# Moving register loads behind a run's output matmuls, and dropping a copy at the end of a sort, in a gather-scatter kernel

## The chip, the cores and the metric

The kernel runs on one core of one Trainium2 chip. The metric is the device time of the whole program in microseconds (us). Before the change it was 990.08 us (median of 3 runs, 989.51 to 990.09).

Two clocks appear. The views of the profile count from the start of the span. Raw records of the trace carry an offset of 10.5 us: where the prediction says "load 673.60 to 674.87", the views have 663.05 to 664.32. Its "565 to 570 us" is also on the raw clock.

## The reference

There are 4096 nodes with 256 features and 262144 edges. Each edge adds its source's transformed features to its destination.

```python
N, E, D = 4096, 262144, 256
self_out = nodes @ w_self
msg = nodes[edges_src] @ w_msg
agg = np.zeros((N, D)); np.add.at(agg, edges_dst, msg)
return self_out + agg
```

## The kernel before

The kernel sorts the edges by keys of destination segment (512 nodes), source block (128 nodes), destination and source, all on VectorE with some transposes on PE. The sorted edges lie in 2048 columns of 128. One "run" is one pair of destination segment and source block: 8 segments x 32 blocks = 256 runs, about 8 columns each. For each column VectorE makes two one-hot tiles, and PE multiplies them into a count matrix in PSUM (the `ring`). Where in the ring a column lands depends on the data, so the address comes from a register, loaded from SBUF. Each run also has one head matmul at a fixed address, which opens its place in the ring, so a run has nine ring matmuls. When a run is complete, ScalarE copies its 128x512 counts to SBUF (`at`), and four output matmuls multiply them with the transformed features `Y`.

```python
LAG = 10
...
    def count_mm(ap, e, d, ci, start, after=()):          # one column into the ring
        mm = nc.tensor.matmul(out=ap, lhsT=e[...], rhs=d[...], start=start, stop=True, ...)
    def evac(r):                                          # ring -> at, on ScalarE
        ins = nc.scalar.copy(out=at[:], in_=ring[:, b:b + SEGW]).ins
    def apply_run(r):                                     # the output matmuls of run r
        s, b = divmod(r, T)
        if b == 0:  ...                                   # 8 more matmuls open a segment (self term)
        for t in range(SEGW // P):                        # 4 of them
            nc.tensor.matmul(
                out=out_ps[:, t, :], lhsT=at[:, t * P:(t + 1) * P], rhs=Y[:, b, :],
                start=False, stop=(b == T - 1), skip_group_check=True,
            )
        if b == T - 1:                                    # a segment ends
            o_sb = ohp.tile([P, SEGW // P, D], FP32, name="o_sb", tag="o_sb", bufs=2)
            for t in range(0, SEGW // P, 2):
                nc.scalar.copy(out=o_sb[:, t:t + 2, :], in_=out_ps[:, t:t + 2, :])
                nc.sync.dma_start(out_v[s, :, t:t + 2, :], o_sb[:, t:t + 2, :])
...
        for c in range(NCOL):
            ...                                           # one-hots for 16 columns; head matmul of a run
            if c % 8 == 0:
                regs = [nc.tensor.alloc_register(f"po{c}_{i}") for i in range(8)]
                nc.tensor.load(regs, poffs[0:1, c:c + 8])
            off = nc.tensor.snap(regs[c % 8], donate=True, min_val=0, max_val=RING * SEGW - W)
            count_mm(ring[:, bass.ds(off, W)], e, d, ci, False)
            while nev < NRUN and (8 * nev + 7 + MARG <= c or c == NCOL - 1):
                evac(nev)
                todo.append((c + LAG, nev))
                nev += 1
            while todo and (todo[0][0] <= c or c == NCOL - 1):
                apply_run(todo.pop(0)[1])
```

A run's evacuation is issued at column 1 of a later group of eight. With a lag of 10 its output matmuls follow column 3 of a group. With 14 they follow column 7, so the next instruction is the load for the next eight columns.

Of the kernel before, what the change touches and what calls it, by code (L numbers as in the profile page):

```python
# [21 lines left out]
SL = 16  # L22
RING = 6
MARG = 10
LAG = 10
NRUN = 256
SENT = float((1 << 24) - 1)

# [7 lines left out]
def _view3(ap: bass.AP, inner: int):  # L36
    return ap.rearrange("p (a b) -> p a b", b=inner)
# [3 lines left out]
def kernel(  # L41
# [9 lines left out]
    nc = tc.nc  # L51
# [4 lines left out]
    NCOL = E // P  # L56
# [3 lines left out]
    NSTAGE = 18  # L60
    JBITS = 11
    G16 = NCOL // P
# [14 lines left out]
    ident = const.tile([P, P], FP32, name="ident")  # L77
# [8 lines left out]
    XA = [sortp.tile([P, NCOL], FP32, name=f"XA{i}") for i in range(2)]  # L86
    XB = [sortp.tile([P, NCOL], FP32, name=f"XB{i}") for i in range(2)]

    HC = NCOL // 2
    for h in range(2):  # L90
# [17 lines left out]
            out=key, in0=dlo, scalar=128.0, in1=slo, op0=ALU.mult, op1=ALU.add  # L108
        )
        nc.vector.scalar_tensor_tensor(  # L110
            out=key, in0=dhi, scalar=float((1 << 21) - (1 << 16)), in1=key,
# [3 lines left out]
            out=key, in0=shi, scalar=float((1 << 16) - P), in1=key,  # L115
# [24 lines left out]
        out=hbase[:], in0=hbase[:], scalar1=float(SEGW), scalar2=None, op0=ALU.mult  # L140
# [6 lines left out]
        out=thr[:], in0=thr[:], scalar1=float(SEGW), scalar2=-0.5, op0=ALU.mult, op1=ALU.add  # L147
# [31 lines left out]
    for t in range(T):  # L179
        y_ps = psum_y.tile([P, D], FP32, name="y_ps", tag="y_ps", bufs=2)  # L180
        for k in range(2):
            nc.tensor.matmul(  # L182
                out=y_ps[:], lhsT=XT[:, k, t * P:(t + 1) * P], rhs=wcat[:, 2 + k, :],
# [2 lines left out]
        nc.scalar.copy(out=Y[:, t, :], in_=y_ps[:])  # L186

    psum_sort = tc.alloc_tile_pool(name="psum_sort", bufs=1, space=bass.MemoryType.PSUM)
    _run_sort(nc, psum_sort, XA, XB, ident, NCOL, NSTAGE, JBITS, G16)
    srt = XA[0]  # L190
    lane = XB[0]


    k16 = meta.tile([P, G16], FP32, name="k16")
# [26 lines left out]
        out=ex[:], in0=dl[:], scalar1=float(W - SEGW), scalar2=0.0, op0=ALU.add, op1=ALU.max  # L221
# [9 lines left out]
        out=wr[:], in0=sl[:], scalar1=float(RING), scalar2=float(-RING * SEGW),  # L231
# [3 lines left out]
        out=wr[:], in0=sl[:], scalar=float(SEGW), in1=wr[:], op0=ALU.mult, op1=ALU.add  # L235
# [20 lines left out]
    for h in range(2):  # L256
        nc.scalar.activation(
            out=junk[:], in_=gball[:], func=ACTF.Sign, bias=thr[:, h:h + 1], scale=-1.0,
# [3 lines left out]
        out=cnt[:], in0=cnt[:], scalar1=0.5, scalar2=float(NCOL // 2 - 1), op0=ALU.mult, op1=ALU.add  # L262
    )
    nc.vector.tensor_scalar(
        out=cidx[:], in0=cnt[:], scalar1=0.0, scalar2=None, op0=ALU.max
# [5 lines left out]
    for h in range(2):  # L271
        xh = meta.tile([P, P], FP32, name=f"xh{h}")
        nc.gpsimd.indirect_dma_start(
            out=xh[:], out_offset=None, in_=xs_dram[:, :],
# [61 lines left out]
    def evac(r):  # L336
        at = ohp.tile([P, SEGW], BF16, name="at", tag="at", bufs=4)
        b = (r % RING) * SEGW
        ins = nc.scalar.copy(out=at[:], in_=ring[:, b:b + SEGW]).ins  # L339
        tc.declare_no_dep(  # L340
            ins, group="count", keep=[last_mm[0]], reason="disjoint banks by static schedule"
        )
        tc.add_manual_dep(ins, last_mm[0].name, DEP, reason="run complete")
        tc.add_to_no_dep_group("evac", ins)
        evac_of[r] = ins
        at_of[r] = at
# [28 lines left out]
    with tc.manual_schedule():  # L375
# [5 lines left out]
        for c in range(NCOL):  # L381
# [19 lines left out]
# [4 lines that stand above are left out]
# [18 lines left out]
        out=hh[:], in0=rho[:], scalar1=float(SEGW), scalar2=float(SEGW), op0=ALU.mult, op1=ALU.add  # L423
    )
    nc.vector.scalar_tensor_tensor(
        out=v[:], in0=gn[:], scalar=1.0, in1=hh[:], op0=ALU.add, op1=ALU.min
# [3 lines left out]
        out=bad[:], in0=v[:], scalar=float(W), in1=bad[:], op0=ALU.is_gt, op1=ALU.add  # L430
# [3 lines left out]
        out=bad[:], in0=v[:], scalar=float(W - 1), in1=bad[:], op0=ALU.is_gt, op1=ALU.add  # L434
# [4 lines left out]
        out=bad[0:1, 0:1], in0=gi[0:1, 0:1], scalar=float(W - 1), in1=bad[0:1, 0:1],  # L439
# [71 lines left out]
def _run_sort(nc, psum, XA, XB, ident, NCOL, NSTAGE, JBITS, G16):  # L511

    cur = {"A": 0, "B": 0}

    def buf(lay):
        return XA[cur[lay]][:, 0:NCOL] if lay == "A" else XB[cur[lay]][:, 0:NCOL]

    def other(lay):
        return XA[1 - cur[lay]][:, 0:NCOL] if lay == "A" else XB[1 - cur[lay]][:, 0:NCOL]

    def flip_live(lay):
        cur[lay] = 1 - cur[lay]

    def evac(out_ap, in_ap, g):
        if g % 2 == 0:
            nc.scalar.copy(out=out_ap, in_=in_ap)  # L526
        else:
            nc.vector.tensor_copy(out=out_ap, in_=in_ap)

    def switch_A_to_B():  # L530
        src = buf("A")
        dst3 = buf("B").rearrange("q (p g) -> q p g", g=G16)
        for g in range(G16):
            tp = psum.tile([P, P], FP32, name="tp_sw", tag="tp", bufs=4)
            nc.tensor.transpose(tp[:], src[:, g * P:(g + 1) * P], ident[:])  # L535
            evac(dst3[:, :, g], tp[:], g)

    def switch_B_to_A():
        src3 = buf("B").rearrange("q (p g) -> q p g", g=G16)
        dst = buf("A")  # L540
        for g in range(G16):
            tp = psum.tile([P, P], FP32, name="tp_sw2", tag="tp", bufs=4)
            nc.tensor.transpose(tp[:], src3[:, :, g], ident[:])
            evac(dst[:, g * P:(g + 1) * P], tp[:], g)

    def flip(lay, blo, bhi):
        x = buf(lay)
        if lay == "A":
            assert blo <= JBITS - 1 and (bhi is None or bhi <= JBITS - 1)
            base_lo = blo  # L550
        else:
            assert blo >= 7
            base_lo = blo - 7
            if bhi is not None:
                assert bhi == blo + 1
        if bhi is None:
            per = 1 << (base_lo + 1)
            reg = _view3(x, per)[:, :, (1 << base_lo):per]
        else:
            per = 1 << (base_lo + 2)  # L560
            reg = _view3(x, per)[:, :, (1 << base_lo):(3 << base_lo)]
        nc.vector.tensor_scalar(out=reg, in0=reg, scalar1=-1.0, scalar2=None, op0=ALU.mult)

    def cpass(lay, fb):
        src = buf(lay)
        dst = other(lay)
        per = 1 << (fb + 1)
        s3 = _view3(src, per)
        d3 = _view3(dst, per)
        lo_s = s3[:, :, 0:(1 << fb)]  # L570
        hi_s = s3[:, :, (1 << fb):per]
        lo_d = d3[:, :, 0:(1 << fb)]
        hi_d = d3[:, :, (1 << fb):per]
        nc.vector.tensor_tensor(out=lo_d, in0=lo_s, in1=hi_s, op=ALU.min)  # L574
        nc.vector.tensor_tensor(out=hi_d, in0=lo_s, in1=hi_s, op=ALU.max)  # L575
        flip_live(lay)

    for s in range(1, NSTAGE + 1):
        if s <= JBITS - 1:
            if s == 1:  # L580
                flip("A", 1, None)
            else:
                flip("A", s - 1, s)
            for b in range(s - 1, -1, -1):
                cpass("A", b)
        else:
            switch_A_to_B()
            if s == NSTAGE:
                flip("B", NSTAGE - 1, None)
            else:  # L590
                flip("B", s - 1, s)
            for b in range(s - 1, 6, -1):
                cpass("B", b - 7)
            switch_B_to_A()
            for b in range(6, -1, -1):
                cpass("A", b)

    if cur["A"] != 0:
        nc.vector.tensor_copy(out=XA[0][:, 0:NCOL], in_=XA[cur["A"]][:, 0:NCOL])
        cur["A"] = 0  # L600
    switch_A_to_B()
    if cur["B"] != 0:
        nc.vector.tensor_copy(out=XB[0][:, 0:NCOL], in_=XB[cur["B"]][:, 0:NCOL])
        cur["B"] = 0


# [28 lines left out]
```

## Time and profile before

| stage | span (us) | what limits it |
|---|---|---|
| sort | 0 to 517 | VectorE, 92 to 98% busy by stretch from 40 us on |
| sorted keys to first count matmul | 517 to 548 | a chain of small work and DMAs |
| count loop, 256 runs | 548 to 979 | see below |
| tail | 979 to 988 | last copies, output, flag |

First, the table by stretch of the loop: start and end, length, then busy us (and instructions) of PE, PE weight load, VectorE, ScalarE, GpSimd, then the granted clock, the DMA share and GB/s.

```profile
700.00:800.00 100.00, 74.67 (x792) 60.46 (x790) 70.01 (x68) 36.92 (x64) 0.00 (x0) 1.00 0.04 12
```

Nothing is full in these 100 us. The clock is at full speed and DMA is nearly idle. The timeline of PE shows what a run looks like (start, us, engine, line, operation, count, and in brackets the idle time before it).

```profile
701.87 0.38 PE L323 MATMUL ring<-d_oh,e_oh 128*128 128x96 bf16 x5
702.66 0.57 PE L323 MATMUL ring<-d_oh,e_oh 128*128 128x96 bf16 x4 [0.41 <-issue]
703.07 0.60 PE L365 MATMUL out_ps<-Y,at 128*128 128x256 bf16 x4
703.50 0.38 PE L323 MATMUL ring<-d_oh,e_oh 128*128 128x96 bf16 x5
704.29 0.57 PE L323 MATMUL ring<-d_oh,e_oh 128*128 128x96 bf16 x4 [0.41 <-issue]
```

A run takes 1.63 us, with a gap of 0.41 us before its first four ring matmuls. "issue" means that PE waited for nothing that the profile shows. It is tempting to read it as "the load takes 0.41 us too long". The view by source line has the instructions that the busy times leave out: those of PE's own sequencer (marked q). Columns: engine, operation, count, shortest/median/longest in ns, first and last start.

```profile
L396 PEldq TENSOR_LOAD <-poffs x256: 587/591/1332, 548.2 to 977.7; - x128
L323 PEldq FUSED_REGOPS  x474: 37/37/37, 700.0 to 799.5; - x158
```

There is one load per run, of 0.59 us. There is one register computation per count matmul (the trace calls it FUSED_REGOPS), of 0.037 us. The starts of one run's sequencer instructions, from the raw records, show how they follow each other (ns from the load's start):

```
load 0 (588 long) | register computations at 689 804 919 1044 | 1159 1279 1394 1509 | next load about 115 later
                                          columns 0  1   2   3      4    5    6    7
```

The pitch is 0.115 us, with or without the four output matmuls between columns 3 and 4. 0.590 + 0.100 + 8 x 0.115 = 1.61 us is the undisturbed run; the mean period between loads is 1.685 us. The records close the gap to the mean: over 256 runs the loads take 4.8 us more than 0.590 us each, and the other intervals are in sum 14.3 us longer than 0.100 and 0.115 us each, mostly small stalls; 1.610 + (4.8 + 14.3) / 256 = 1.685. The sequencer hardly rests.

The end of the sort, in the chain of waits, that is the work that ended last, followed back from the end (start, us, what):

```profile
516.06 1.15 DVE XA_85 L575
517.23 1.24 DVE XA_84 L599
518.49 0.19 DVE k16i L217
```

These are the last pass of the sort, the copy, and the first work that needs the sorted keys. The copy is in the chain.

### The profile page before, as it was taken

The numbers are of one execution on the slowest core, as the hardware profiler recorded it, in microseconds if no ns is written. First come the engines' busy times: TensorE is split into PE (matmuls) and PEld (weight loads), VectorE is DVE, ScalarE is ACT, GpSimd is POOL, SyncE is SP. The second block draws the span as 40 slices with busy tenths as digits, with TensorE's granted clock in tenths as the row PEclk, the third lists the DMA queues.
The fourth block names the chain that finished last, engine by engine and source line by source line (L and its number), as shares of the span: only waits on it lengthen the run. The fifth ranks groups of instructions, "written<-read, shape, count | busy, mean of one in ns | idle before, by whom it ended". The sixth has DMA issues, their size and how long they took to land.

```text
span 988.2 us, 11711 instructions
## 1 busy us (share of the span) xinstructions
PE 417.9 (42%) x3730; PEld 317.9 (32%) x3730; DVE 782.6 (79%) x851; ACT 222.0 (22%) x449; POOL 14.3 (1%) x24
## 2 busy tenths in 40 slices
PE   0033301131111120202012677777777777777775
PEld 0000001121111120101011566565565656566654
DVE  3999999989999989898995986767766666767640
ACT  0011101021010110101003233333333333333333
POOL 4000000000000000000000000000000000000000
PEclk9999999999555555555555699999999999999999
DMA  8611100000000000000003000000000000000000
GB/s 228 132 26 26 24 0 0 1 1 0 0 0 0 0 1 0 0 0 0 0 0 93 1 2 23 1 23 1 1 23 2 23 1 23 2 23 1 23 2 24
DMA packets 25217, 18.03 MB, mean 18 GB/s; under 512 B 11557, under 2 KB 24358, under 8 KB 24390
## 3 DMA queue, kind: packets, MB, share of 16 engines
q1 hardware_dynamic: 19862, 11.59, 3.9%
q0 software_dynamic: 4720, 2.49, 1.9%
q10 hardware_dynamic: 578, 3.16, 0.8%
q8 instruction: 39, 0.64, 0.3%
q14 instruction: 18, 0.15, 0.0%
HBM read 10.12 MB, written 7.37 MB: 18 GB/s over the span
## 4 chain that ended last, share of the span: by engine, by line
DVE 49%; PE 35%; issue 12%; DMA 3%; ACT 0%; DVEq 0%; ACTq 0%; SPq 0%
PE ring L323 18%; PE out_ps L365 10%; DVE XA_85 L574 7%; DVE XA_84 L574 7%; DVE XA_85 L575 7%; DVE XA_84 L575 6%; DVE XB_86 L574 4%; DVE XB_87 L574 4%; DVE XB_87 L575 3%; DVE XB_86 L575 3%; PE tp_sw L535 3%; DVE e_oh L307 2%; DVE d_oh L307 2%; DMA XB_86<-in_edges_dst_dram 2%; DMA fd<-bcol 1%
## 5 line engine op out<-in xcount | busy, mean ns | idle before, releaser
L323 PE MATMUL ring<-d_oh,e_oh 128*128 128x96 bf16 x2304 | 242.3, 206 | 114.9 <-issue 105.0
L307 DVE TENSOR_TENSOR e_oh<-slo_b,jrow 128x2048 bf16<-128x2048 bf16 x128 | 156.5, 1222 | 114.1 <-PE ring L323 114.1
L323 PEld LDWEIGHTS <-e_oh 128*128 128x128 bf16 x2304 | 170.2, 98 | 158.9 <-issue 143.5
L339 ACT CAST at<-ring 128x512 bf16<-128x512 f32 x256 | 150.0, 586 | 289.9 <-PE ring L323 289.9
L365 PE MATMUL out_ps<-Y,at 128*128 128x256 bf16 x1024 | 154.3, 273 | 0.2 <-ACT at L339 0.2
L307 DVE TENSOR_TENSOR d_oh<-rel_b,jrow 128x1536 bf16<-128x1536 bf16 x128 | 121.7, 951 | 0.0
L365 PEld LDWEIGHTS <-at 128*128 128x128 bf16 x1024 | 85.0, 97 | 15.9 <-issue 1.8
L574 DVE TENSOR_TENSOR XA_85<-XA_84 128x1024 f32<-128x1024 f32 x56 | 68.6, 1225 | 2.2
L574 DVE TENSOR_TENSOR XA_84<-XA_85 128x1024 f32<-128x1024 f32 x55 | 67.4, 1225 | 2.2
L575 DVE TENSOR_TENSOR XA_85<-XA_84 128x1024 f32<-128x1024 f32 x56 | 68.3, 1219 | 0.0
L575 DVE TENSOR_TENSOR XA_84<-XA_85 128x1024 f32<-128x1024 f32 x55 | 67.1, 1219 | 0.0
L182 PE MATMUL y_ps<-wcat,XT 128*128 128x256 bf16 x64 | 25.2, 395 | 97.5 <-DMA XT<-nodes_bf_dram 97.5
L535 PE MATMUL tp_sw<-ident,XA_84 128*128 128x128 f32 x80 | 20.6, 432 | 88.1 <-DVE XA_84 L575 68.9
L535 PE MATMUL tp_sw<-ident,XA_85 128*128 128x128 f32 x64 | 15.8, 436 | 93.7 <-DVE XA_85 L575 93.7
L535 PEld LDWEIGHTS tp_sw<-ident,XA_84 128*128 128x128 f32 x80 | 14.1, 192 | 94.5 <-DVE XA_84 L575 70.0
L182 PEld LDWEIGHTS <-XT 128*128 128x128 bf16 x64 | 6.7, 104 | 115.7 <-DMA XT<-nodes_bf_dram 115.7
L535 PEld LDWEIGHTS tp_sw<-ident,XA_85 128*128 128x128 f32 x64 | 11.6, 190 | 97.8 <-DVE XA_85 L575 52.4
L526 ACT COPY XB_86<-tp_sw 128x128 f32<-128x128 f32 x40 | 15.1, 377 | 119.4 <-PE tp_sw L535 116.9
L574 DVE TENSOR_TENSOR XB_87<-XB_86 128x1024 f32<-128x1024 f32 x30 | 36.8, 1225 | 1.0
L574 DVE TENSOR_TENSOR XB_86<-XB_87 128x1024 f32<-128x1024 f32 x30 | 36.8, 1225 | 1.0
L575 DVE TENSOR_TENSOR XB_87<-XB_86 128x1024 f32<-128x1024 f32 x30 | 36.6, 1219 | 0.0
L575 DVE TENSOR_TENSOR XB_86<-XB_87 128x1024 f32<-128x1024 f32 x30 | 36.6, 1219 | 0.0
(478 smaller groups left out, 288.3 us busy)
## 6 DMA issues: line engine op xcount, KB each, us to landing
out_dram<-o_sb SPq DMA_DIRECT2D x16, 256.0 KB, 2.5
XB_87<-in_edges_src_dram ACTq DMA_DIRECT2D x2, 1024.0 KB, 8.7
XB_86<-in_edges_dst_dram SPq DMA_DIRECT2D x2, 1024.0 KB, 8.5
nodes_bf<-in_nodes_dram POOLq DMA_DIRECT2D x1, 2048.0 KB, 20.1
nodes_bf_dram<-nodes_bf SPq DMA_DIRECT2D x1, 2048.0 KB, 8.7
XT<-nodes_bf_dram SPq DMA_TRANSPOSE x64, 2.4
xs_dram<-XA_84 ACTq DMA_DIRECT2D x1, 1024.0 KB
gball<-gd SPq DMA_DIRECT2D x1, 1024.0 KB, 4.7
```

What stands on the lines that cost most here:

```text
L182: nc.tensor.matmul(out=y_ps[:], lhsT=XT[:, k, t * P:(t + 1) * P], rhs=wcat[:, 2 + k, :], start=(k == 0), stop=(k == 1),)
L307: tt(out=o[:], in0=val.rearrange("p (g i) -> p g i", i=2).unsqueeze(2).to_broadcast(shp), in1=jrow[:, 0:wid, :].unsqueeze(1).to_broadcast( ...
L323: mm = nc.tensor.matmul(out=ap, lhsT=e[:, ci // 2, :, ci % 2], rhs=d[:, ci // 2, :, ci % 2], start=start, stop=True, skip_group_check=True ...
L339: ins = nc.scalar.copy(out=at[:], in_=ring[:, b:b + SEGW]).ins
L365: nc.tensor.matmul(out=out_ps[:, t, :], lhsT=at[:, t * P:(t + 1) * P], rhs=Y[:, b, :], start=False, stop=(b == T - 1), skip_group_check=True,)
L526: nc.scalar.copy(out=out_ap, in_=in_ap)
L535: nc.tensor.transpose(tp[:], src[:, g * P:(g + 1) * P], ident[:])
L574: nc.vector.tensor_tensor(out=lo_d, in0=lo_s, in1=hi_s, op=ALU.min)
L575: nc.vector.tensor_tensor(out=hi_d, in0=lo_s, in1=hi_s, op=ALU.max)
```

## The change

It has two parts. The lag moves each run's output matmuls directly ahead of the next register load, so that PE has work while the load runs. The second part hands on whichever of two buffers holds the sorted data, instead of copying it into the first. For the second array the number of passes is even, so there was no copy to leave out. One copy of 128x2048 f32 goes.

```diff
-LAG = 10
+LAG = 14
...
-    _run_sort(nc, psum_sort, XA, XB, ident, NCOL, NSTAGE, JBITS, G16)
-    srt = XA[0]
-    lane = XB[0]
+    srt, lane = _run_sort(nc, psum_sort, XA, XB, ident, NCOL, NSTAGE, JBITS, G16)
...
-    if cur["A"] != 0:
-        nc.vector.tensor_copy(out=XA[0][:, 0:NCOL], in_=XA[cur["A"]][:, 0:NCOL])
-        cur["A"] = 0
     switch_A_to_B()
-    if cur["B"] != 0:
-        nc.vector.tensor_copy(out=XB[0][:, 0:NCOL], in_=XB[cur["B"]][:, 0:NCOL])
-        cur["B"] = 0
+    return XA[cur["A"]], XB[cur["B"]]
```

## The prediction

> **What bounds the kernel now.** The sort runs until 517 us (VectorE 90 to 100% busy), metadata until 548, then 432 us of count matmuls (256 runs of 8 columns), then a 9 us tail. In the loop no datapath is full: from 700 to 800 us the stage table has PE at 75, VectorE at 70, ScalarE at 37 of 100 us. The timeline repeats: 4 ring matmuls, 4 output matmuls, 5 ring matmuls, a 0.41 us gap called "issue".
>
> The gap looks like an exposed register load, but the trace's records of PE's register instructions, which the page leaves out, show the sequencer itself as the limit. Per run: one TENSOR_LOAD of 8 registers (median 0.590 us), 0.10 us later the first register computation, then 8 of these 0.115 us apart. 0.690 + 8 x 0.115 + 0.005 = 1.615 us; the median period between loads is 1.628, the mean 1.68. The pitch stays 0.115 us across the 4 output matmuls, and while PE is behind with them: the sequencer isn't held by PE. So the Trainium skill (Perfetto Trace Analysis, Sequencer Loop): engine instructions are pushed into a queue, control instructions execute in the sequencer. Loads took 0.587 and 0.590 us with over 1 us of PE work queued (565 to 570 us), and 0.588 to 0.603 with PE nearly idle: the load doesn't wait for PE to drain.
>
> **What the change does.**
> 1. The lag of 14 instead of 10 moves a run's output matmuls from behind column 3 to behind column 7, just ahead of the next load. It removes no sequencer work. They will execute under the load, and the ring matmuls issue one by one, 0.115 us apart. PE's gaps move; the period, a sum of sequencer times, doesn't. The naive gain (0.44 us of output matmuls under the load instead of 0.22 us of ring matmuls, 256 times = 56 us) should not come. Expected: 0 per run.
> 2. Seven loads (one after each of the first seven segments) take 1.20 to 1.33 us instead of 0.59: they coincide with that segment's output transfer, e.g. load 673.60 to 674.87, packets 673.47 to 675.14. Transfers start about 1.81 us after the segment's last output matmul. The load now falls at about 1.5 to 2.1 us after it instead of 1.95; about half collides: estimate 7 x 0.3 = 2 us saved, at worst 0, at best 4.5.
> 3. The copy of the sorted keys (128x2048 f32, VectorE, 1.23 us at 517.23) disappears; the next work (518.49) and the first transpose wait for it. All critical: -1.25 us.
> 4. Tail: the last ring matmul no longer stands behind output matmuls: -0.2 us.
> 5. Instruction fetch stalls (an estimate: about 0.135 us every 7 runs) may fall elsewhere: +-1 us.
>
> **Predicted: 986.4 us**, 80% range 983.6 to 989.4. Chances: faster by over 2% 0.04, within 2% 0.94, slower 0.02.
>
> **What would show it right.** Median period between loads still 1.62 to 1.63 us, load 0.59, pitch 0.115; in the timeline 9 ring matmuls over about 1 us, then 4 output matmuls, then a gap of about 0.3 us; "issue" waits of PE split into more, smaller gaps; loop start 1.25 us earlier; loads behind segment ends under 1.2 us.
>
> **What would make it wrong.** If the load overlaps with dispatch of output matmuls, or the 8 static instructions ahead of it cost sequencer time, the period changes by up to 0.1 us = 26 us either way. If the load must wait for output matmuls directly ahead, it grows to over 0.7 us: 30 us slower. If PE's new pattern lowers the granted clock, slower.

## The result, and the profile after

The changed kernel took 985.79 us (median of 4 runs, 984.66 to 986.21), against 990.09 us before (4 runs) on the same chip. The ratio is 0.9956, with a 95% interval of 0.9939 to 0.9973. Ratios here are the mean time of one kernel's runs over that of the other's of the same rounds, so they are not quite the ratio of the medians quoted. By the 2% measure the two are the same, but the interval leaves out 1: a gain of about 0.4% is clear of the noise.

The table by stretch, the timeline of PE and the loads, after:

```profile
700.00:800.00 100.00, 88.83 (x795) 68.39 (x793) 70.03 (x69) 36.98 (x64) 0.00 (x0) 1.00 0.04 12
```

```profile
700.33 1.01 PE L321 MATMUL ring<-d_oh,e_oh 128*128 128x96 bf16 x9 [0.18 <-issue]
701.17 0.60 PE L363 MATMUL out_ps<-Y,at 128*128 128x256 bf16 x4
701.96 1.01 PE L321 MATMUL ring<-d_oh,e_oh 128*128 128x96 bf16 x9 [0.18 <-issue]
702.80 0.60 PE L363 MATMUL out_ps<-Y,at 128*128 128x256 bf16 x4
```

```profile
L394 PEldq TENSOR_LOAD <-poffs x256: 587/590/934, 547.4 to 973.5; - x128
L321 PEldq FUSED_REGOPS  x480: 37/37/37, 700.2 to 799.8; - x160
```

The gap called "issue" shrank from 0.41 to 0.18 us per run, and PE's busy time in these 100 us rose from 74.67 to 88.83 us. Yet PE did the same work at the same rate: 792 matmuls before, 795 after. PE's waits in the same stretch (who waited for what: total us, times, longest) say it once more, before and then after:

```profile
PE ring L323 <- issue: 24.3, 57, 0.5
```

```profile
PE ring L321 <- issue: 10.9, 58, 0.5
```

More than half of the visible idle time is gone, 13.4 us in 100, and the loop is no faster for it. Nine ring matmuls in 1.01 us are spread out one by one, at the 0.115 us of the sequencer. Each ring matmul's record covers some 0.205 us, while bunched ones start only 0.044 us apart. So matmuls spread in time look like a busy engine, while bunched ones overlap in the records. The Trainium skill (Perfetto Trace Analysis, before the section Sequencer Loop) calls matmul busy time a bad metric because matmuls are pipelined. This trace agrees, with 14 us more "busy" for the same matmuls.

The end of the sort in the chain of waits, after:

```profile
515.53 1.14 DVE XA_85 L573
516.66 0.10 DVE k16i L215
```

The copy is gone from the chain. Where the 4.5 us of the two profiled spans (988.2 and 983.7 us) came from, by differences of the records:

| piece | before | after | gain (us) |
|---|---|---|---|
| start to first count matmul | 548.15 | 547.39 | 0.76 |
| first load to last register computation | 431.14 | 427.62 | 3.52 |
| of that: 256 loads, at a mean of 0.6089 and 0.6006 us | 155.9 | 153.8 | 2.1 |
| rest of the loop | 275.3 | 273.9 | 1.4 |
| last register computation to the end | 8.91 | 8.70 | 0.2 |

The rest of the loop, 1.4 us, is about 0.4 us in the first nine runs, mostly at half clock, and about 1.2 us in small differences of a few ns: before, the interval right behind the output matmuls (between columns 4 and 5) had a median of 0.120 us, after the change the median is 0.115 us for every column. Other differences cancel. Why those 5 ns exist I do not know.

### The profile page after: what moved, and what is told of

The parts are those of the page before. It is cut to its first block, busy times and chain, and to the rows that moved or that the text cites. A ratio compares the mean times of both kernels' runs of the same rounds, so it can differ in the third digit from the quotient of the medians.

```text
span 983.7 us, 11709 instructions
## 1 busy us (share of the span) xinstructions
PE 477.3 (49%) x3730; PEld 349.9 (36%) x3730; DVE 780.3 (79%) x850; ACT 221.1 (22%) x449; POOL 14.2 (1%) x24
## 4 chain that ended last, share of the span: by engine, by line
DVE 48%; PE 43%; issue 6%; DMA 3%; ACT 0%; DVEq 0%; SPq 0%
PE ring L321 25%; PE out_ps L363 11%; DVE XA_85 L572 7%; DVE XA_84 L572 7%; DVE XA_85 L573 7%; DVE XA_84 L573 6%; DVE XB_86 L572 4%; DVE XB_87 L572 4%; DVE XB_87 L573 3%; DVE XB_86 L573 3%; PE tp_sw L533 3%; DMA XB_86<-in_edges_dst_dram 2%; DVE e_oh L305 1%; DVE d_oh L305 1%; DMA fd<-bcol 1%
## 5 line engine op out<-in xcount | busy, mean ns | idle before, releaser
L321 PE MATMUL ring<-d_oh,e_oh 128*128 128x96 bf16 x2304 | 262.8, 206 | 52.1 <-issue 50.0
L321 PEld LDWEIGHTS <-e_oh 128*128 128x128 bf16 x2304 | 202.6, 97 | 128.1 <-issue 98.8
```

Of the source, the lines that this page charges most:

```text
L321: mm = nc.tensor.matmul(out=ap, lhsT=e[:, ci // 2, :, ci % 2], rhs=d[:, ci // 2, :, ci % 2], start=start, stop=True, skip_group_check=True ...
```

## The experiments

Ten kernels were run. All gave correct results but one.

### One part at a time

The first has only the change to the sort, the second only the lag.

```diff
# copy_only, against the changed kernel
-LAG = 14
+LAG = 10
# lag_only, against the kernel before
-LAG = 10
+LAG = 14
```

> The copy at the end of the sort left out, the lag kept at 10. My theory (the copy is on the critical path, the rest of the gain is the lag): 1.0 to 1.3 us under the kernel before, so 988.8 to 989.1 us; the loads behind the segments' ends still 1.20 to 1.33 us long. Rival (all of the gain is the copy and what it sets off): about 985.8 us, as the changed kernel.

> The lag of 14, the copy kept. My theory: about 3.3 us under the kernel before, 986.4 to 987.2 us; the seven loads behind the segments' ends 0.86 to 0.94 us instead of 1.20 to 1.33; median period between loads about 1.62 us. Rival (the moved loads hide nothing and cost nothing): 990.1 us.

Leaving out the copy alone: 987.76 us (5 runs, 986.83 to 988.94) beside 989.35 us before, ratio 0.9986, interval 0.9972 to 1.000. The lag alone: 986.53 us (5 runs, 985.72 to 989.5), ratio 0.9970, interval 0.9957 to 0.9984. So the copy is worth 1.4 us and the lag 3.0 us, and together they make the 4.3 us of the whole. The copy's interval reaches 1, so its gain alone is not clear of the noise; a gain of 1.0 to 1.3 us was expected. The expected time, 988.8 to 989.1 us, was missed by 1 us, in part because the kernel before ran at 989.35 us in these rounds and not at 990.09. Medians of single kernels scatter by 1 to 2 us, so the copy's share is known to about that only. The lag alone has a loop of 427.67 us in its profile and the copy alone one of 430.71, against 427.62 and 431.14 for the changed kernel and the one before. (The profiled run of the lag alone was its slowest, 989.5 us, with 3 us more in the sort; only its loop is compared.) Six of the seven long loads of the copy alone stayed at 1.20 us or more; one was 0.87. With the lag alone all were 0.87 to 0.94 us, as expected.

### Does PE's work set the period?

```diff
-                out=out_ps[:, t, :], lhsT=at[:, t * P:(t + 1) * P], rhs=Y[:, b, :],
+                out=out_ps[:, t, 0:64], lhsT=at[:, t * P:(t + 1) * P], rhs=Y[:, b, 0:64],
```

> Wrong result on purpose: the changed kernel, whose output matmuls process 64 columns instead of 256; the number and order of instructions stay. My theory (PE's sequencer sets the period of the loop): median period between loads still 1.61 to 1.62 us; the time within 2 us of the changed kernel (984 to 986 us, the start and the tail may win about 1 us). Rival (PE's matmul time plus an exposed rest of the load sets it): each run 4 x 0.08 = 0.32 us shorter, 256 runs, so about 903 us.

984.66 us (4 runs), ratio 0.9955 to the kernel before, and wrong (relative error 0.86). With a quarter of the columns in 1024 output matmuls the kernel is as fast as the changed one, within about 1 us. The timeline and the table by stretch:

```profile
700.96 1.07 PE L321 MATMUL ring<-d_oh,e_oh 128*128 128x96 bf16 x9 [0.34 <-issue]
701.84 0.41 PE L363 MATMUL out_ps<-Y,at 128*128 128x64 bf16 x4
702.59 1.07 PE L321 MATMUL ring<-d_oh,e_oh 128*128 128x96 bf16 x9 [0.34 <-issue]
```

```profile
700.00:800.00 100.00, 78.06 (x799) 67.19 (x798) 70.47 (x68) 37.05 (x65) 0.00 (x0) 0.53 0.04 12
```

The period is still 1.63 us, and only the gap grew, to 0.34 us. The last columns hold a surprise: with nothing changed but the columns of the output matmuls, the granted clock fell from 1.00 to 0.53 in this stretch. So PE's own time did not shrink as planned, and the 903 us of the rival, worked out at full clock, is not what it would give here. At half clock bunched ring matmuls start about 0.080 us apart instead of 0.044, and output matmuls 0.054 instead of 0.109. By these spacings (an estimate) PE needs 9 x 0.080 + 4 x 0.054 = 0.94 us per run instead of 0.83: a loop bound by PE's work would have become some 27 us longer. It did not. The clock records of this run also have stretches at full clock, of 3.4 us (one of 6.8); there the same four matmuls start 0.028 us apart, and by the same estimate PE needs some 0.3 us less per run than in the changed kernel:

```profile
665.45 0.28 PE L363 MATMUL out_ps<-Y,at 128*128 128x64 bf16 x4
667.07 0.28 PE L363 MATMUL out_ps<-Y,at 128*128 128x64 bf16 x4
```

The ten periods that fit into these stretches are no shorter (1.617 to 1.745 us; the shortest at half clock is 1.616). PE's work is not the bound, neither in amount nor in clock, and the rival falls. VectorE is not the bound either: in the changed kernel its only waits from 600 to 900 us are for PE's ring matmuls (90.3 us in 78 waits), and by the records it finishes a one-hot tile 22 us (median) before PE uses it.

### Does the load's time add to the period?

The number of registers per load was changed in the changed kernel.

```diff
-            if c % 8 == 0:
-                regs = [nc.tensor.alloc_register(f"po{c}_{i}") for i in range(8)]
-                nc.tensor.load(regs, poffs[0:1, c:c + 8])
+            if c % NREG == 0:                      # NREG = 4, 16 or 32
+                regs = [nc.tensor.alloc_register(f"po{c}_{i}") for i in range(NREG)]
+                nc.tensor.load(regs, poffs[0:1, c:c + NREG])
-                regs[c % 8], donate=True, ...
+                regs[c % NREG], donate=True, ...
```

> The changed kernel with one load of 16 registers every two runs, instead of one of 8 every run. My theory: the load's sequencer time adds to the period, so halving the number of loads shortens the loop by 128 times their fixed part. If a load is all per-register time (0.59 / 8 = 0.074 us each), only the 0.10 us behind each load is saved: 13 us, about 973 us. If it is nearly all fixed: 128 x 0.69 = 88 us, about 898 us. I expect about half of it, 935 us. Rival (the load is hidden behind the output matmuls in the changed kernel and costs only the 0.17 us gap of PE): at most 128 x 0.17 = 22 us, not under 964 us.

> The changed kernel with one load of 4 registers twice per run. My theory: a load of 4 takes 0.076 + 4 x 0.064 = 0.33 us; 256 more loads cost 256 x 0.176 = 45 us: 1027 to 1034 us. Rival (the load behind the output matmuls is hidden behind them): only the second load of each run costs, and the first one, shorter by 0.26 us, gains: under 1000 us.

> The changed kernel with one load of 32 registers every four runs. Loads of 8 took 0.590 us and of 16 took 1.104 us: 0.064 us per register and 0.076 us fixed, and 0.10 us behind each. My theory: a load of 32 takes 0.076 + 32 x 0.064 = 2.13 us; 64 fewer loads than with 16 save 64 x 0.176 = 11 us, less 3 to 5 us lost as PE and VectorE run in longer bursts: 963 to 969 us. Rival (the load's cost is hidden when it is rarer): under 940 us.

The loads of the three kernels, with 4, 16 and 32 registers:

```profile
L395 PEldq TENSOR_LOAD <-poffs x512: 326/328/827, 547.4 to 1021.3; - x171
```

```profile
L395 PEldq TENSOR_LOAD <-poffs x128: 1101/1104/1994, 546.9 to 959.5; - x128
```

```profile
L395 PEldq TENSOR_LOAD <-poffs x64: 2127/2131/3027, 547.2 to 957.1; - x64
```

A load takes 0.328, 0.590, 1.104 and 2.131 us for 4, 8, 16 and 32 registers. That is close to 0.07 us plus 0.064 us per register. It is mostly per register, so my guess for 16 registers ("about half", 935 us) was far off. The 972.87 us measured lie at one end of the bracket given with it, and they do not decide by themselves: the rival (not under 964 us) allows them too. The times of the four:

| kernel | time (us) | loads | load + 0.10 + matmuls at 0.115, per two runs | loop per two runs, measured |
|---|---|---|---|---|
| 4 registers | 1032.62 (1 run, state unknown) | 512 | 4 x 0.428 + 1.84 = 3.55 | 3.71 |
| 8 (the changed kernel) | 985.79 | 256 | 2 x 0.690 + 1.84 = 3.22 | 3.34 |
| 16 | 972.87 (ratio 0.9834, 0.9819 to 0.9849) | 128 | 1.204 + 1.84 = 3.04 | 3.25 |
| 32 | 974.68 (ratio 0.9851, 0.9829 to 0.9874) | 64 | 1.115 + 1.84 = 2.96 | 3.25 |

The run with 4 registers is the sharpest: two loads per run instead of one cost 47 us, as the sum says (256 x 0.176 = 45), although one load of each pair still stands directly behind the output matmuls. Nothing of it is hidden, and the rival (under 1000 us) falls. With 16 registers the loop gained 12.1 us where the sum has 22.5 (128 x 0.176); the last experiment finds where most of the rest went.

The run with 32 registers missed its expectation, 963 to 969 us. Its sum is lower than with 16, its loop is not. In the table by stretch for the whole loop, with 16 and then with 32 registers, the column of the clock differs:

```profile
560.00:970.00 410.00, 313.71 (x3294) 257.88 (x3291) 279.74 (x272) 154.22 (x267) 0.00 (x0) 0.99 0.04 12
```

```profile
560.00:970.00 410.00, 312.14 (x3294) 263.96 (x3291) 278.71 (x273) 154.44 (x267) 0.00 (x0) 0.90 0.04 12
```

PE idles about 2 us while 32 registers load, and the granted clock drops to half for 3.4 us at a time. In such a stretch PE falls behind:

```profile
743.19 1.08 PE L322 MATMUL ring<-d_oh,e_oh 128*128 128x96 bf16 x9 [1.71 <-DVE d_oh L306]
744.11 1.01 PE L364 MATMUL out_ps<-Y,at 128*128 128x256 bf16 x4
744.92 0.93 PE L322 MATMUL ring<-d_oh,e_oh 128*128 128x96 bf16 x9
745.65 1.05 PE L364 MATMUL out_ps<-Y,at 128*128 128x256 bf16 x4
```

Four output matmuls last 1.01 and 1.05 us here instead of 0.60. In the raw records the sequencer then waits 0.37 to 0.65 us longer before a load, while PE works off its backlog. The interval before the load is 0.115 us when undisturbed; over the whole loop it exceeds that by 16.1 us in sum. The seven segment changes (see below) have 8.0 us of it, five of them at full clock. Another 7.3 us are 13 waits elsewhere; before each of them the clock had been at half for over 3 of the last 4.5 us, and of the other loads away from the segment changes only one had that, near the loop's start. That the clock causes these 13 is argued from this coincidence; no run isolates it. Note also the bracket "1.71 <-DVE d_oh": VectorE had finished that tile 21 us before by the records (at 722.06), so the wait was for the sequencer's load, which the releaser's inference cannot see.

### Why seven loads took twice as long

```diff
# hold_out, against the kernel before
-            o_sb = ohp.tile([P, SEGW // P, D], FP32, name="o_sb", tag="o_sb", bufs=2)
+            o_sb = ohp.tile([P, SEGW // P, D], FP32, name="o_sb", tag="o_sb", bufs=8)
-                nc.sync.dma_start(out_v[s, :, t:t + 2, :], o_sb[:, t:t + 2, :])
+                held.append((s, t, o_sb))
...   # behind the loop; the last segment's transfer is first in the queue and holds the others
+        for s, t, o_sb in reversed(held):
+            nc.sync.dma_start(out_v[s, :, t:t + 2, :], o_sb[:, t:t + 2, :])
# lag12, against the changed kernel
-LAG = 14
+LAG = 12
```

> The kernel before, with eight output buffers instead of two and all output transfers held back until the last segment is done. My theory (the seven loads of 1.20 to 1.33 us are slowed by the output transfer that runs at the same time): no load over 0.7 us but the first; the loop, from first load to last register computation, 431.1 - 4.4 = about 426.7 us. The whole is slower, since 4 MB then leave at the end (about 12 us more, some 997 us). Rival (the eight extra matmuls of a new segment, or the wait for the copies out of PSUM, hold the load): seven loads of 1.2 us as before, loop 431 us.

> The changed kernel with a lag of 12: output matmuls behind column 5. By the time at which a load begins, against the output transfer behind it: with the lag of 10 it begins 0.14 us after the transfer's packets and took 1.20 to 1.33 us; with 14, about 0.3 us before them, and took 0.87 to 0.93. My theory: in between, 1.0 to 1.2 us; median period between loads within 0.01 us of 1.63; time 987 us. Rival (what counts is the load standing directly behind output matmuls): 1.2 us or more, as with the lag of 10.

The loads with the transfers held back, and then those with a lag of 12:

```profile
L398 PEldq TENSOR_LOAD <-poffs x256: 587/590/784, 548.7 to 973.9; - x128
```

```profile
L394 PEldq TENSOR_LOAD <-poffs x256: 587/590/1471, 547.5 to 976.5; - x128
```

Without output transfers in the loop no load is long but the first (0.784 us, long in every kernel with 8 registers). The loop took 426.69 us, as expected (426.7), and the whole 996.98 us (one run, state unknown), because 4 MB then leave at the end. So the transfer is the cause (its issue and its packets were moved together; the times below point to the packets). The rival, the new segment's extra matmuls and their wait, was present unchanged in this kernel and lengthened no load.

The lag of 12 gave 988.53 us (one run, state unknown) and seven loads of 0.89 to 1.47 us, five of them at 1.39 or more. I expected 1.0 to 1.2. So "half the overlap, half the loss" is only rough. With the lag of 14 a load begins about 0.3 us before the transfer's packets, overlaps them for about 0.6 us and takes 0.87 to 0.93 us. With 10 it begins 0.07 to 0.16 us behind their start and takes 1.20 to 1.33. With 12 it mostly begins 0.03 to 0.08 us before them, overlaps fully, and takes up to 1.47. By the records a load is lengthened by 0.5 to 0.6 of the time for which it overlaps packets with lags of 10 and 14, and mostly by 0.6 or a little more with 12. Why it is more there is open.

### A version that beats both

With 16 registers the sequencer stood 0.78 to 0.90 us too long at each of the seven segment changes: PE waited with the new segment's first matmul for the copies out of PSUM, and the sequencer, unlike in the steady loop, was held behind it. One of them, with the load starting at 604.82:

```profile
604.75 1.03 PE L359 MATMUL out_ps<-wcat,XT 128*128 128x256 bf16 x8 [0.66 <-ACT o_sb L371]
```

A lag of 22 puts the load between the old segment's last output matmuls and the new one's first. The second kernel tests the sum in another way: half the registers, but one more register operation per matmul.

```diff
# reg16_lag22, against the kernel with 16 registers
-LAG = 14
+LAG = 22
# pack16_lag22, against reg16_lag22
+    nc.vector.scalar_tensor_tensor(
+        out=pk[:], in0=poff[:, 1::2], scalar=4096.0, in1=poff[:, 0::2], op0=ALU.mult, op1=ALU.add)
...
-                nc.tensor.load(regs, poffs[0:1, c:c + NREG])               # 16 registers
+                nc.tensor.load(regs, poffs[0:1, c // 2:(c + NREG) // 2])   # 8 registers
+            if c % 2 == 0:
+                both = nc.tensor.snap(regs[c % NREG // 2], ...)
+            off = both % 4096 if c % 2 == 0 else both // 4096              # (with its bounds)
```

> One load of 16 registers every two runs, and a lag of 22, so that the load falls between the last run of a segment and the first of the next one. In the run with 16 registers and a lag of 14 the sequencer stood 0.78 to 0.90 us at each of the seven segment changes, as PE waited for the copies out of PSUM with the new segment's matmuls, and seven loads took up to 1.99 us instead of 1.10. My theory: the wait falls into the load (7 x 0.8 = 5.6 us saved) and the load is over before the transfer begins, the next one overlaps its end only (3 to 5 us saved): 962 to 966 us. Rival (the sequencer's sum alone counts, wherever the load stands): 972 to 973 us.

> As the kernel before it, with two offsets packed in one 32-bit word: a load of 8 registers every two runs instead of 16, and one more register operation (a remainder or a division) for each of the 16 count matmuls. Per two runs the load gets 8 x 0.064 = 0.51 us shorter, and each matmul's register instruction, now 0.037 us for two operations, longer. Theory (all sequencer time adds up): break-even is 0.032 us per added operation; an operation at the mean of the present two (0.018 us) would save 0.22 us per two runs, 28 us; twice the break-even costs 65 us. Whatever the added length in the trace, the median period between loads must change by 16 times it less 0.51 us. Rival (register instructions are hidden behind PE's matmuls): 0.51 us saved per two runs, about 900 us.

The lag of 22 with 16 registers took 965.4 us (4 runs, 964.67 to 965.98), ratio 0.9748 to the kernel before, interval 0.9725 to 0.9771. It beats both kernels, and the rival (972 to 973 us) falls. Its loads, and PE's table by stretch:

```profile
L395 PEldq TENSOR_LOAD <-poffs x128: 1101/1105/1382, 546.8 to 952.1; - x128
```

```profile
700.00:800.00 100.00, 79.48 (x836) 65.14 (x833) 73.19 (x71) 39.04 (x67) 0.00 (x0) 1.00 0.04 12
```

The longest load fell from 1.99 to 1.38 us, and the loop from 415.6 to 408.3 us. By the records 4.3 us of these 7.3 are loads. The waits at the segment changes, 6.0 us, are gone as well, but some 3 us of small stalls came in their place. The loop is now 19.3 us shorter than the changed kernel's, of the 22.5 us of the sum. PE does 836 matmuls in 100 us instead of 792, with less "busy" time than the changed kernel.

The packed version took 980.98 us (4 runs; ratio 0.9907, interval 0.9883 to 0.9930), far from the rival's 900 us. Its register computations:

```profile
L326 PEldq FUSED_REGOPS  x483: 75/78/79, 700.0 to 800.0; - x161
```

Each is 0.041 us longer, above the break-even of 0.032. The sum says 16 x 0.041 - 0.51 = +0.14 us per two runs; the median period went from 3.176 to 3.325 us, +0.149. The load fell to 0.591 us, and more than that was paid back in arithmetic. Register computations are not hidden behind matmuls either.

## Why the prediction was right

The predicted time was 986.4 us, the measured 985.79, inside 983.6 to 989.4. That range is wider than the gain itself, so the number alone only rules out the larger effects that the prediction names (26, 30 and 56 us). That it came within 0.6 us is partly luck, as the points show. The mechanism rests on the experiments. By point:

1. *The period does not move.* Right. The quartiles (within 6 ns), the load and the pitch stayed, while PE's gap fell from 0.41 to 0.18 us (0.3 was predicted). The prediction also had more gaps; there were 57 before and 58 after in 100 us. The naive 56 us did not come. The prediction gave 1.628 us as the median period before; that was a slip of reading, it is the lower quartile, and the median is 1.638, after the change 1.635. The tests of the cause are the run with thin output matmuls (the same period at full and at half clock), the loads of 4 registers and the packed offsets. The prediction's "the sequencer isn't held by PE" holds for the steady loop only: at segment changes with 16 registers it was held for up to 0.90 us. The Trainium skill (Perfetto Trace Analysis, Sequencer Loop) says that engine instructions go into a queue and control instructions are executed in the sequencer; the records of the steady loop agree (pitch 0.115 us across four output matmuls).
2. *The collisions.* The cause was right (held-back transfers: no long load) and the sum as well: 2.1 us from the loads, 2 predicted. The long loads shrank from 1.20 to 1.33 us to 0.87 to 0.93. But that the sum fits to 0.1 us is luck in part. The loads fell 1.49 to 1.56 us after the segment's last output matmul, at the early end of the predicted 1.5 to 2.1. With the lag of 12 they mostly fell about 1.75 us after it, in the middle of that range, and five of the seven were longer than any before the change.
3. *The copy.* -1.25 us was predicted and -1.4 us measured when it was left out alone (interval 0 to -2.8). In the one pair of profiles the loop starts only 0.76 us earlier (1.29 us in the profile of the copy alone), although the last pass of the sort happened to end 0.5 us earlier. The time went into DMA waits between the sort and the loop, which vary from run to run: the small transfer of `bcol` in the chain took 7.09 us before and 7.63 after. A single pair of profiles could not have settled a point of 1 us.
4. *The tail.* -0.2 us predicted; from the last register computation to the last matmul it went from 1.92 to 1.85 us, and to the end of the span from 8.91 to 8.70. The size fits, but one pair of profiles is too little to judge.
5. *Fetch stalls.* The stalls of about 0.135 us every 7 runs are in both kernels, about as many of them, at other places in the run (34 of 0.13 to 0.14 us before, 35 after). That they are fetches fits the DMA records: nearly all are followed, 0.9 to 1.3 us later, by a packet of the queue called "instruction".

Not foreseen were some 1.2 us from intervals that are 5 ns shorter each. They are the main term that makes the loop 3.5 us faster instead of 2.

## What to carry to other kernels

In this kernel an "issue" gap on PE was a place where PE waited for its sequencer, not a latency to be covered. Where you see one, add up the sequencer's own instructions over one period (loads, register computations, register-addressed matmuls) and see whether they fill it. If they do, moving PE's work about is likely to give next to nothing, and doing fewer or shorter sequencer instructions is what helps: here twice the registers per load, and a load placed where PE has to wait anyway, gave 2.5% where the reordering gave 0.4%. And do not take a rise of PE's busy time as progress when the number of matmuls per us has not moved.

## What the Trainium skill lacked or had wrong

- No page gives the cost of a register load from SBUF on PE by the number of registers. DMA: Bandwidth & Descriptors (Latency and other measured facts) has a floor of about 600 ns for `tensor_load`, without the number of registers or the source; loads of 4 registers took 0.328 us here, so it is no floor for these. Runtime: NRT & Kernel Launch (Instruction fetch mechanics) has about 200 ns per register for loads described as being from HBM; here, from SBUF, the runs show 0.328, 0.590, 1.104 and 2.131 us for 4, 8, 16 and 32 registers, about 0.064 us each, and 0.10 us before the next instruction.
- No page that I read says that a register load is slowed by a DMA transfer at the same time: 0.59 us became up to 1.47 us beside an output transfer, and of 256 without it only the first took over 0.60 (0.784 us).
- TensorE: Matmul & The Clock Gate (Step-by-step) gives about 62 ns of sequencer time per matmul with hardware decode off. A matmul with a register address plus its computation held the sequencer for 0.115 us here, and 0.156 us with one more register operation. It does not treat this case.
- The same page (What's actually happening) says that the clock follows how busy PE has been, and names as the condition for half rate at least one idle window of about 3.4 us. Here it was 0.90 on average with idle gaps of about 2 us (32 registers), and 0.53 for thin output matmuls with gaps of 0.34 us that came every 1.63 us; PE was nowhere idle for 3.4 us in either loop. So the amount of work, not only a whole idle window, seems to count; no run isolates the rule.
